# The last step of an encoder block: where the scale factors of the second half lie, and how the output is grouped

## The chip, the cores and the metric

The kernel runs on one core of a Trainium2 chip. The metric is the device time of one execution in microseconds. The core has five engines that the profile names: TensorE (PE; its weight loads are PEld), VectorE (DVE), ScalarE (ACT), GpSimd (POOL) and SyncE (SP, which here only issues transfers). Each has its own queue of instructions and they meet through semaphores.

## The reference

One layer of an encoder with a sequence of 512 and a width of 1024, in float32. A gated convolution and an attention branch are merged, a channel mixer follows, and a last RMS norm ends it. Cut to what the change touches:

```python
def rms_norm(x, g):
    x32 = x.astype(jnp.float32)
    y = x32 * lax.rsqrt(jnp.mean(x32 * x32, axis=-1, keepdims=True) + EPS)
    return y.astype(x.dtype) * g

def reference(x, ...):
    ...                       # branches, merge, norm, up projection and its convolution
    a, b = jnp.split(up, 2, axis=-1)
    x = x + (jax.nn.silu(a) * b) @ w_down[l]
    return rms_norm(x, norm_f_g)
```

The change is in the last line: each position's 1024 values are multiplied by the reciprocal root of their mean square.

## The kernel before

The sequence lies along the free dimension, the width along the partitions: `x1` holds eight slabs of 128 x 512. Nearly the whole program is matrix products on TensorE, each as three passes of rounded high and low parts (`mm3`, line 283; `passes`, line 301). A planner orders the instructions of an engine by their readiness, except those wrapped in `keep`, which stay in the written order among themselves on their engine. It also puts in the semaphores, and it lets only one engine at a time read or write a bank of PSUM, so that two readers of one tile in PSUM follow each other. PSUM has eight banks, called by number through `bank(i, name)`.

The end of the program works on two halves of the sequence, of 256 positions each: t = 0 and t = 1 (`halves[t]`). Slabs 0 to 5 are finished by then for both. Slabs 6 and 7 of the down projection are computed last, in the order slab 6 and 7 of the first half (`pdA`), then slab 6 and 7 of the second half (`pdB`). For each half these steps follow:

- `fin_sum` (lines 1208 to 1211): VectorE adds the product to `x1` (for the last slab of the second half the residual is already in PSUM), ScalarE takes the square and then scales the slab by the norm's weights.
- `fin_col` (line 1216) and `rstd_col` (lines 344 to 352): the squares are summed over the partitions by matmuls with a column of ones into bank 2 (first half) or 3 (second half), `pc_n` in the trace; ScalarE takes the root, VectorE the reciprocal, `rc_n`.
- `rstd_bc` (line 363): TensorE spreads the 256 reciprocal roots over all partitions, with an identity matrix, into bank 1 (first half) or 4 (second half), `pb_n` in the trace.
- `fin_out` (lines 1219 to 1232): VectorE multiplies slabs 0 to 5 with the factors in PSUM, in four instructions over 1, 2, 2 and 1 slabs. GpSimd, which works from a copy in SBUF, multiplies slabs 6 and 7; ScalarE makes that copy, `rs`. The output leaves in five transfers. In the first half SyncE issues all of them; in the second ScalarE issues the second and third.

Written out, the order at the end is:

```python
    plain7(1, 1, kall[3:6])
    fin_out(0, rcA)
    plain7(1, 1, kall[6:])
    sqB.append(fin_sum(1, 1))
    warm_on(3)
    rcB = fin_col(1, sqB)
    warm_on(6)
    fin_out(1, rcB)
```

So the first half's output stands in front of the last products of the second half. `warm_on` gives TensorE matmuls whose results are not used, into bank 5. On ScalarE the first half's copy `rs`, on line 1227, stands ahead of the square of the last slab, on line 1210. Line 1352 in the trace is the closing sequence of the program: SyncE waits for all transfers, every engine drains its own queue, and the engines exchange semaphores.

Of the kernel before, what the change touches and what calls it, by code (L numbers as in the profile page):

```python
# [10 lines left out]
AF = mybir.ActivationFunctionType  # L11
ALU = mybir.AluOpType

P = 128
D = 1024
S = 512
# [46 lines left out]
def block_kernel(ctx, tc, xT, vecs, wv, win, wmix, wo, wup, wst, wdp, outT):  # L63
# [3 lines left out]
    nc = tc.nc  # L67
# [6 lines left out]
    def keep(ins):  # L74
        return tc.keep_in_program_order(ins)

    def bank(i, name):
        return ps.tile([P, S], F32, tag=f"b{i}", name=name)
# [280 lines left out]
    def rstd_bc(rc, n, bb, name):  # L359

        pb = bank(bb, f"pb_{name}")
        for t in range(n):
            keep(nc.tensor.matmul(
                pb[:, t * P : (t + 1) * P], rc[:, t : t + 1].to_broadcast([P, P]), ident,
                start=True, stop=True,
            ))
        return pb
# [59 lines left out]
    pb = [pb_[t // 2][:, (t % 2) * 4 * HD : (t % 2 + 1) * 4 * HD] for t in range(NT)]  # L427
# [277 lines left out]
    z, e, o = (ap.tile([n, S], F32, tag="pp", name=nm, bufs=NPP) for nm in ("fz", "fe", "fo"))  # L705
# [71 lines left out]
    for i in range(n + LA):  # L777
# [10 lines left out]
        if 0 <= i - LA < n:  # L788
            pr, e, qb = units[i - LA]
# [72 lines left out]
    for j in range(KB):  # L862
# [28 lines left out]
        a, b = gs  # L891
# [8 lines left out]
    x1 = xp.tile([P, KB, S], F32, tag="x1", name="x1")  # L900
# [317 lines left out]

    def fin_out(t, rc):
        hs = halves[t]  # L1220
        pb = rstd_bc(rc, 2, (1, 4)[t], f"n3{t}")[:, : S // 2]
        rs = fp.tile([P, S], F32, tag="fu", name=f"rs{t}", bufs=3)[:, : S // 2]
        parts_ = ((0, 1), (1, 3), (3, 5), (5, 6), (6, 8))
        for a, b in parts_[:4]:
            y = x1[:, a:b, hs]
            keep(nc.vector.tensor_mul(y, y, pb.unsqueeze(1).to_broadcast([P, b - a, S // 2])))
        keep(nc.scalar.activation(rs, pb, AF.Copy))
        y = x1[:, 6:8, hs]
        keep(nc.gpsimd.tensor_mul(y, y, rs.unsqueeze(1).to_broadcast([P, 2, S // 2])))
        for g in (0, 1, 2, 3, 4):  # L1230
            a, b = parts_[g]
            keep((nc.sync, nc.scalar)[t * (g in (1, 2))].dma_start(outT[:, a:b, hs], x1[:, a:b, hs]))

    def warm_on(n):

# [10 lines left out]
    rcA = fin_col(0, sqA)  # L1246
# [10 lines that stand above are left out]
# [100 lines left out]
```

## Time and profile before

| | |
|---|---|
| time, median of 3 runs | 700.87 us (700.78 to 701.2) |
| profiled execution, its own time | 700.85 us |
| span of its trace | 699.1 us |
| TensorE busy | 688.4 us (98%) |
| VectorE, ScalarE, GpSimd busy | 506.6, 346.6, 159.6 us |
| transfers | 118.91 MB, mean 170 GB/s |
| mean granted TensorE clock | 0.996 |

Times in the trace count from the start of the span, in microseconds. A row of a timeline has the start, the length, the engine, the line, the operation, what it writes and reads, the shape and how many instructions are merged in it; in square brackets stands how long the engine was idle before it and who ended that. Lengths of merged rows reach from the first to the last of them. A row of a line or tile has the shortest, median and longest instruction in ns and when the first and the last began. "q" behind an engine's name means its instruction queue, which also issues the transfers.

### The profile page before, as it was taken

What the parts mean: (1) busy time and instruction counts of PE and PEld (TensorE: products, weight loads), DVE (VectorE), ACT (ScalarE), POOL (GpSimd) and SP (SyncE); (2) the same over time, 40 slices, a digit from 0 to 9 for tenths busy, and PEclk for the clock granted to TensorE, in tenths of its full rate; (3) what the DMA queues carried; (4) which work ended last, traced back from release to release, by engine and by line L of the source; (5) the groups of instructions that cost most, each with busy time, mean ns of one, the idle gap of its engine ahead of it and who ended that gap; (6) DMA issues with size and microseconds to landing.
All of it is one profiled execution on the core that took longest, in us unless ns stands there. A gap on an engine that the chain in (4) does not pass through costs nothing.

```text
span 699.1 us, 14571 instructions
## 1 busy us (share of the span) xinstructions
PE 688.4 (98%) x5978; PEld 686.1 (98%) x5978; DVE 506.6 (72%) x806; ACT 346.6 (50%) x551; POOL 159.6 (23%) x180
## 2 busy tenths in 40 slices
PE   9999999999999999999999999999999999999994
PEld 9999999999999999999999999999999999999994
DVE  6678777786687777764577877777775677877783
ACT  5574656555664443543445443455443345444662
POOL 5124646434011001035221212220000221200001
PEclk9999999999999999999999999999999999999998
DMA  8527877567359868758566647588675554334513
GB/s 313 184 85 204 206 153 186 132 167 177 96 143 272 254 179 241 233 183 206 144 156 175 168 111 214 144 182 224 192 225 178 147 147 99 102 99 139 161 60 121
DMA packets 54466, 118.91 MB, mean 170 GB/s; under 512 B 4960, under 2 KB 24416, under 8 KB 54400
## 3 DMA queue, kind: packets, MB, share of 16 engines
q1 hardware_dynamic: 39104, 96.55, 43.0%
q0 software_dynamic: 14576, 20.75, 18.6%
q8 instruction: 47, 0.77, 0.4%
q10 hardware_dynamic: 720, 0.69, 0.3%
q14 instruction: 19, 0.16, 0.1%
HBM read 115.80 MB, written 35.13 MB: 216 GB/s over the span
## 4 chain that ended last, share of the span: by engine, by line
PE 95%; DVE 2%; ACT 1%; issue 1%; ACTq 0%; POOLq 0%; POOL 0%; DVEq 0%
PE p_up L283 26%; PE p_in L283 14%; PE dn L301 13%; PE gs L301 8%; PE p_up L301 8%; PE p_wo L283 6%; PE yc L301 3%; PE ya L283 3%; PE pa L491 2%; PE pb L493 2%; PE p_g L283 2%; PE o L672 2%; PE tp L657 1%; PE pdA L283 1%; PE pdB L283 1%
## 5 line engine op out<-in xcount | busy, mean ns | idle before, releaser
L283 PE MATMUL p_up<-x1h,wh_up 128*128 128x256 f32 x536 | 104.8, 277 | 0.0
L283 PE MATMUL p_up<-x1l,wh_up 128*128 128x256 f32 x536 | 104.4, 276 | 0.0
L283 PE MATMUL p_up<-x1h,wl_up 128*128 128x256 f32 x536 | 104.3, 276 | 0.0
L250 ACT ACTIVATE wh_up<-raw_up 128x1024 fp32r<-128x1024 f32 x44 | 46.6, 1060 | 83.8 <-PE p_up L283 74.5
L139 POOL DMA_DIRECT2D sum<-in_wst_dram x51 | 52.7, 1108 | 125.3 <-DMA sum<-sum 89.1
L283 PEld LDWEIGHTS p_up<-x1h,wh_up 128*128 128x128 f32 x536 | 80.7, 188 | 0.5 <-issue 0.5
L283 PEld LDWEIGHTS p_up<-x1l,wh_up 128*128 128x128 f32 x536 | 80.8, 188 | 0.0
L283 PEld LDWEIGHTS p_up<-x1h,wl_up 128*128 128x128 f32 x536 | 80.6, 188 | 0.0
L254 DVE TENSOR_TENSOR wl_up<-raw_up,wh_up 128x1024 fp32r<-128x1024 f32 x44 | 54.1, 1230 | 16.1 <-ACT wh_up L250 16.1
L250 ACT ACTIVATE wh_F<-raw_F 128x1024 fp32r<-128x1024 f32 (+1 forms) x32 | 33.6, 1049 | 58.2 <-PE ya L283 25.9
L283 PE MATMUL p_in<-xgh,wh_in 128*128 128x256 f32 x288 | 56.8, 279 | 0.0
L283 PE MATMUL p_in<-xgh,wl_in 128*128 128x256 f32 x288 | 56.5, 277 | 0.1
L283 PE MATMUL p_in<-xgl,wh_in 128*128 128x256 f32 x288 | 56.4, 277 | 0.0
L989 DVE TENSOR_TENSOR fz<-p_up,rb_n 128x512 f32<-128x512 f32 x44 | 30.3, 690 | 32.4 <-PE p_up L283 32.4
L254 DVE TENSOR_TENSOR wl_F<-raw_F,wh_F 128x1024 fp32r<-128x1024 f32 (+1 forms) x32 | 38.6, 1207 | 20.0 <-ACT wh_F L250 19.3
L283 PEld LDWEIGHTS p_in<-xgh,wh_in 128*128 128x128 f32 x288 | 44.7, 188 | 0.7
L1002 POOL TENSOR_TENSOR ge<-fu,fu 128x512 f32<-128x512 f32 x11 | 17.1, 1552 | 120.2 <-DVE fu L586 107.2
L283 PEld LDWEIGHTS p_in<-xgh,wl_in 128*128 128x128 f32 x288 | 43.5, 188 | 0.3 <-DVE wl_in L254 0.3
L283 PEld LDWEIGHTS p_in<-xgl,wh_in 128*128 128x128 f32 x288 | 43.6, 188 | 0.0
L250 ACT ACTIVATE wh_P<-raw_P 128x768 fp32r<-128x768 f32 (+1 forms) x32 | 26.6, 832 | 27.3 <-PE dn L301 15.0
L301 PE MATMUL p_up<-x1h,wh_up 128*128 128x256 f32 x168 | 40.2, 276 | 0.0
L301 PE MATMUL p_up<-x1l,wh_up 128*128 128x256 f32 x168 | 40.2, 276 | 0.0
(319 smaller groups left out, 2033.1 us busy)
## 6 DMA issues: line engine op xcount, KB each, us to landing
raw_up<-in_wup_dram SPq DMA_DIRECT2D x44, 512.0 KB, 4.4
raw_F<-sum SPq DMA_DIRECT2D x31, 512.0 KB, 4.9
raw_in<-in_win_dram SPq DMA_DIRECT2D x24, 512.0 KB, 4.6
raw_P<-in_wst_dram SPq DMA_DIRECT2D x31, 384.0 KB, 3.6
sum<-in_wst_dram POOLq DMA_DIRECT2D x31, 256.0 KB, 5.7
sum<-in_wst_dram SPq DMA_DIRECT2D x15, 512.0 KB, 6.1
sum<-in_wst_dram POOLq DMA_DIRECT2D x15, 512.0 KB, 8.0
sum<-sum SPq DMA_DIRECT2D x30, 256.0 KB, 6.4
```

Of the source, the lines that this page charges most:

```text
L139: return lambda: keep(nc.gpsimd.dma_start(dst, src, accum_op=ALU.add))
L250: ins = nc.scalar.activation(hi, raw, AF.Copy)
L254: ins = nc.vector.tensor_sub(lo, raw, hi.bitcast(F32))
L283: keep(nc.tensor.matmul(out[:, cs], w, x[:, cs], start=start and i == 0 and c == 0, stop=stop and i == 2 and c == len(cut) - 1,))
L301: keep(nc.tensor.matmul(out, wl if x == 1 else wh, xl if x == 2 else xh, start=opens and bk not in seen, stop=closes and bk not in left,))
L491: keep(nc.tensor.matmul(pa[t][:, :VW], xt, w[:, :VW], start=start, stop=stop))
L493: keep(nc.tensor.matmul(pb[t], xt, w[:, VW:], start=start and t % 2 == 0, stop=stop and t % 2 == 1))
L657: keep(nc.tensor.transpose(tp[:, ks], pt[:, ks], ident))
L672: keep(nc.tensor.matmul(o[:, os_], vv[:, kb, pr, e, :], x[:, kb, cs], start=e == 0 and kb == 0 and i == 0, stop=e == 1 and kb == nk - 1 an ...
L989: nc.vector.tensor_mul(z, p, rb2)
L1002: keep(nc.gpsimd.tensor_mul(ge, a.rearrange(halves_of, h=2), b.rearrange(halves_of, h=2)))
```

## The change

`fin_out` is rewritten. In the second half the reciprocal roots are spread twice, into bank 4 for VectorE and into bank 2 for ScalarE's copy; in the first half both still read bank 1, but the copy stands in front of the multiplications instead of behind them. VectorE multiplies slabs 0 to 5 in three instructions over two slabs each. The output leaves in four transfers of two slabs. In the second half SyncE issues the first and third and ScalarE the second and fourth.

```diff
     def fin_out(t, rc):
         hs = halves[t]
-        pb = rstd_bc(rc, 2, (1, 4)[t], f"n3{t}")[:, : S // 2]
+        bks = ((1, 1), (4, 2))[t]
+        pb = rstd_bc(rc, 2, bks[0], f"n3{t}")[:, : S // 2]
+        pr = rstd_bc(rc, 2, bks[1], f"n3{t}r")[:, : S // 2] if t else pb
         rs = fp.tile([P, S], F32, tag="fu", name=f"rs{t}", bufs=3)[:, : S // 2]
-        parts_ = ((0, 1), (1, 3), (3, 5), (5, 6), (6, 8))
-        for a, b in parts_[:4]:
-            y = x1[:, a:b, hs]
-            keep(nc.vector.tensor_mul(y, y, pb.unsqueeze(1).to_broadcast([P, b - a, S // 2])))
-        keep(nc.scalar.activation(rs, pb, AF.Copy))
-        y = x1[:, 6:8, hs]
-        keep(nc.gpsimd.tensor_mul(y, y, rs.unsqueeze(1).to_broadcast([P, 2, S // 2])))
-        for g in (0, 1, 2, 3, 4):
-            a, b = parts_[g]
-            keep((nc.sync, nc.scalar)[t * (g in (1, 2))].dma_start(outT[:, a:b, hs], x1[:, a:b, hs]))
+
+        def by(e, r, g):
+            y = x1[:, 2 * g : 2 * g + 2, hs]
+            keep(e.tensor_mul(y, y, r.unsqueeze(1).to_broadcast([P, 2, S // 2])))
+
+        def copy():
+            keep(nc.scalar.activation(rs, pr, AF.Copy))
+
+        if t == 0:
+            copy()
+        for g in range(3):
+            by(nc.vector, pb, g)
+        if t:
+            copy()
+        by(nc.gpsimd, rs, 3)
+        for g in range(4):
+            keep((nc.sync, nc.scalar)[t * (g % 2)].dma_start(
+                outT[:, 2 * g : 2 * g + 2, hs], x1[:, 2 * g : 2 * g + 2, hs]
+            ))
```

## The prediction

> **What bounds the kernel now.** I read the page first, then the chain of waits for the last 20 us, then each engine's timeline there.
>
> ```profile
> span 699.1 us, 14571 instructions
> ...
> PE 95%; DVE 2%; ACT 1%; issue 1%; ACTq 0%; POOLq 0%; POOL 0%; DVEq 0%
> ```
>
> For 95% of the span TensorE is the path, and the diff touches none of that. Everything is decided in the tail, which the chain of waits shows (start, length, what):
>
> ```profile
> 685.11 0.46 PE pb_n L363 x4
> ...
> 688.10 1.28 POOL x L1229
> 689.38 3.34 issue
> 692.72 1.30 POOLq L1352
> ```
>
> The chain follows GpSimd to the end of the program (L1352 is the closing sequence), not a transfer. What the end waits for is in the rows of L1352 (the first two from 694 us on, the third from 698.3) and in a table of windows (last two columns: share of the DMA engines, GB/s):
>
> ```profile
> L1352 SPq DRAIN  x2: 7/7/7, 696.5 to 696.6; - x2
> L1352 POOLq DRAIN  x1: 5555/5555/5555, 692.7 to 692.7; - x1
> ...
> L1352 POOLq EVENT_SEMAPHORE  x4: 17/17/17, 698.3 to 699.0; - x4
> ...
> 695.00:695.50 0.50, 0.00 (x0) 0.00 (x0) 0.00 (x0) 0.00 (x0) 0.00 (x0) 0.50 1.04 373
> 695.50:695.90 0.40, 0.00 (x0) 0.00 (x0) 0.00 (x0) 0.00 (x0) 0.00 (x0) 0.50 0.46 156
> ```
>
> Output packets stop near 695.8, SyncE has seen them all by 696.6, and GpSimd's drain ends at 692.72 + 5.555 = 698.27. The final exchange of semaphores follows from 698.3 on and ends at 699.07, 0.80 later. So the drain, not the output, is last, by 1.67 us. I call the two halves of the sequence A (t = 0) and B (t = 1).
>
> **The change, step by step.** The rows of ScalarE, TensorE and VectorE:
>
> ```profile
> 687.64 0.38 ACT L1227 ACTIVATE rs<-pb_n 128x256 f32<-128x256 f32 x1 [3.40 <-DVE x L1226]
> 687.92 0.38 ACT L1210 ACTIVATE sq<-pdB 128x256 f32<-128x256 f32 x1
> 688.18 0.48 ACT L1211 ACTIVATE x<-pdB,vec 128x256 f32<-128x256 f32 x1
> 688.99 0.26 ACT L350 ACTIVATE ms_n<-pc_n,ex 128x2 f32<-128x2 f32 x1 [0.33 <-PE pc_n L344]
> 692.29 0.38 ACT L1227 ACTIVATE rs<-pb_n 128x256 f32<-128x256 f32 x1 [3.04 <-DVE x L1226]
> ```
> ```profile
> 682.99 0.50 PE L344 MATMUL pc_n<-ones,ssq 128*128 128x1 f32 x4
> 683.36 0.58 PE L344 MATMUL pc_n<-ones,sq 128*128 128x1 f32 x4
> ...
> 686.68 0.28 PE L283 MATMUL pdB<-gl,wh_dp 128*128 128x256 f32 x1
> ```
> ```profile
> 687.16 0.50 PE L344 MATMUL pc_n<-ones,ssq 128*128 128x1 f32 x4
> 688.35 0.61 PE L344 MATMUL pc_n<-ones,sq 128*128 128x1 f32 x4 [0.69 <-ACT sq L1210]
> ...
> 689.61 0.61 PE L363 MATMUL pb_n<-ident,rc_n 128*128 128x128 f32 x4
> ```
> ```profile
> 689.28 0.17 DVE L352 RECIPROCAL rc_n<-ms_n 128x2 f32<-128x2 f32 x1 [1.74 <-ACT ms_n L350]
> 690.25 1.95 DVE L1226 TENSOR_TENSOR x<-x,pb_n 128x256 f32<-128x256 f32 x4 [0.80 <-PE pb_n L363]
> ```
> ```profile
> 690.59 0.68 DVE L1226 TENSOR_TENSOR x<-x,pb_n 128x512 f32<-128x512 f32 x1
> ...
> 691.19 0.68 DVE L1226 TENSOR_TENSOR x<-x,pb_n 128x512 f32<-128x512 f32 x1
> ```
>
> *1. Half A's copy in front (t = 0).* Before, ScalarE's copy of A waits for VectorE's four multiplications (3.40 us) and holds up B's last square, queued behind it: pdB's last matmul ends at 686.96, the square starts only at 687.92, and TensorE stands 0.69 us for it. Moved ahead, the copy runs when A's roots are ready, at about 685.60 to 685.98; ScalarE is idle then. The price goes to VectorE: one bank, so its multiplications wait for the copy and start at 686.00 instead of about 685.6. Three of 128x512 at a pitch of 0.60 (690.59 to 691.19) end at 686.00 + 2 x 0.60 + 0.68 = 687.88. Queued behind them on VectorE is B's reciprocal; who waits for that is in step 2. A's GpSimd multiplication runs from 686.06 instead of 688.10.
>
> *2. B starts earlier.* The square runs at 687.00 to 687.38; 0.05 later (before: 688.30 to 688.35) TensorE could take it, at 687.43. TensorE is next free at 687.16 + 0.37 = 687.53 (the step from 682.99 to 683.36, half A's same eight matmuls back to back), so it sets the time: sums done at 687.53 + 0.58 = 688.11 instead of 688.96, **0.85 us earlier**. Square root 688.14, reciprocal 688.43 (VectorE is free from 687.88, slack 0.55), B's roots spread from 688.76 to 689.37. Bounds: nothing gained if the square still came late, 0.85 at most since TensorE is then full; I take 0.85, as half A's row shows that pace.
>
> *3. A second bank for B.* The added spread costs TensorE four more matmul records at a pitch of (0.61 - 0.28) / 3 = 0.11, so 0.45 us, behind the first four; VectorE doesn't wait for them. The second bank is ready at 689.82. Bank 2 held half A's column sums (matmuls to 683.94), which nothing reads any more, so it is free. VectorE's three multiplications start 0.03 behind the spread, as before (690.25 against 690.22), at 689.40, and end at 690.08, 690.68 and 691.28. The copy runs at 689.86 to 690.24 instead of at 692.29, beside VectorE's multiplications, and no longer waits for them: the 3.04 us go.
>
> *4. GpSimd's multiplication in B.*
>
> ```profile
> 692.75 1.26 POOL L1229 TENSOR_TENSOR x<-x,rs 128x512 f32<-128x512 f32 x1 [3.38 <-ACT rs L1227]
> 694.04 0.38 SPq L1232 DMA_DIRECT2D out_dram<-x  x1
> ```
> ```profile
> L603 POOL TENSOR_TENSOR z<-z,cc x4: 1292/1294/1295, 68.5 to 163.9; 128x512 f32<-128x512 f32 x4
> ```
> ```profile
> L913 POOL TENSOR_TENSOR ssq<-ssq,sq x7: 1842/1864/1866, 308.3 to 340.9; 128x512 f32<-128x512 f32 x7
> ```
> ```profile
> 105.67 0.70 DVE L633 CUSTOM_DVE_ANT_0 s<-s,strip 128x512 f32<-128x512 f32 x1 [0.23 <-PE s L629]
> ```
> ```profile
> 308.30 0.75 DVE L959 SCALAR_TENSOR_TENSOR x1l<-x,vec,x1h 128x512 fp32r<-128x512 f32 x1
> ```
>
> It starts 0.08 after the copy (692.67 to 692.75), so at 690.32, and now VectorE works beside it. The trace has the same shape at 1.29 (L603, beside VectorE work with one operand in PSUM, such as L633) and at 1.86 (L913, beside L959, whose tensors are all in SBUF). The bounds are 1.26 and 1.86. L1226 reads one operand from PSUM, so L603 is nearest and I keep 1.26: end at 691.58 instead of 694.01, **2.43 us earlier**. With 1.86 it would be 1.83.
>
> The Trainium skill ("GPSIMD Engine Reference", "Key points") says that GpSimd contends with VectorE instructions in a 2-port perf mode or with two SBUF inputs; "SBUF — State Buffer" ("SBUF: two separate sides") calls the shared pair an "exclusive lock". By that rule L1226 takes no lock and the 2.43 stand; a reader who counted L1226 as two-input would get 1.83. L603 and L913 agree with the rule.
>
> *5. Output in four groups of two slabs.* In B the issues follow VectorE's three ends and GpSimd's: SyncE 690.11, ScalarE 690.71, SyncE 691.31, ScalarE 691.61; last before: 694.04. ScalarE's two issues stand behind its copy and hold nothing up. Half A's last issue on SyncE, behind the third (687.92), is over near 688.7, so its packets are through by about 690.4, before B's. A group of 262 KB needs 0.70 us at 373 GB/s. If packets start 0.95 after the issue (694.04 to 695.0, before's last group), four groups run from 691.06 to 693.86 without a gap, so transfers bind there and end 1.9 us earlier than 695.8. SyncE would be done at 694.7 instead of 696.6. Fewer issues (eight, not ten) save nothing on the path.
>
> *6. The end.* The drain ended 4.26 us after GpSimd's multiplication (694.01 to 698.27). If that distance stays, it ends at 691.58 + 4.26 = 695.84, still behind SyncE's 694.7, and the span at 696.64. The bounds of the distance: zero, when SyncE's 694.7 + 0.80 makes 695.5, and no upper one in the trace.
>
> **Sum.** 699.07 - 2.43 = 696.64. The profiled execution took 700.85, 1.75 more than its span of 699.1, and lies 0.02 below the median of 700.87. So 696.64 + 1.75 = **698.4 us**, -0.35%. This kernel's time can be told from no change by about 0.2%, 1.4 us, so from 699.47 down.
>
> **The rivals.**
>
> *The landing sets the drain (0.18).* If GpSimd's drain ends 1.67 us after SyncE has seen the output (696.6 to 698.27), and not by GpSimd's own work, the gain is the transfers' 1.9: **698.95**. For it: transfers ran until 695.8 during the drain. Against: no row shows GpSimd waiting for a transfer there.
>
> *GpSimd and VectorE in each other's way (0.12).* 1.86 instead of 1.26: 0.60 more, **699.0**. L603 speaks against it.
>
> *Half A's copy doesn't come ahead in ScalarE's queue (0.06).* If it is placed behind the last square and its scaling (to 687.74 at the earlier start), the copy ends at 688.1, the multiplications of A at 690.0, the reciprocal behind them at 690.2 and B's roots 1.5 us later than in step 2: **699.9**, no change that can be told. Against: the copy's operands are ready 1.4 us before the square's.
>
> *The change doesn't do what it says (0.04).* If the copy of B still waited for VectorE: VectorE ends at 691.28, copy to 691.75, GpSimd to 693.1, 0.9 gained: **700.0**. The wait before was between two readers of one bank; with two banks I see nothing to make it.
>
> *The drain isn't constant (0.08, both ways).*
>
> ```profile
> L1343 POOLq DRAIN  x1: 177/177/177, 0.3 to 0.3; - x1
> ```
>
> At the start of the program GpSimd's drain took 0.18 us (0.3 to 0.5 us), at the end 5.55; the trace has no third of that kind. If it falls so that SyncE is last, the span is 695.5 and the time **697.2** (0.04). If it grows, for instance since it now starts while more transfers run, the change loses: from 4.26 + 2.43 + 1.4 = 8.1 us after the multiplication the kernel is slower by over 0.2%; a drain twice as long, 11.1 us from 690.28, gives 701.4 + 0.80 + 1.75 = **703.9** (0.04). For it: only that its length is unexplained. Against: transfers ran beside it before as well.
>
> **How the numbers follow.** The forecast has 0.52; landing 0.18, contention 0.12, the shorter and the longer drain 0.04 each, the copy in the wrong place 0.06, no effect 0.04. Faster: 0.52 + 0.18 + 0.12 + 0.04 = 0.86; same 0.06 + 0.04 = 0.10; slower 0.04. The range 697.8 to 699.5 takes in the forecast, landing and contention, and the forecast with only part of step 2 (without it, 699.25); it leaves out both drains, the wrong place and no effect (0.18).
>
> **What would show it.** Right: ScalarE's copy of A at 685.6 with B's square at 687.0; no wait of TensorE for the square; four more pb_n records in B; the copy of B about 0.5 us after VectorE's start; GpSimd's multiplication at 1.26 to 1.3, ending near 691.6; the last issue on ScalarE; the drain about 4.26 after GpSimd. Wrong: the drain ending with SyncE's landing; L1229 in B over 1.6; VectorE's L1226 over 0.68; an ACT copy still released by L1226 in B; or a changed order of instructions ahead of 680 us, which the diff gives no cause for.

## The result, and the profile after

The changed kernel takes **698.46 us** (median of 6 executions, 698.34 to 698.48) against 700.91 us before (6 executions, 700.78 to 701.2). That is 2.45 us less; the ratio is 0.9964, with a 95% interval of 0.9952 to 0.9977. The profiled execution took 698.34 us with a span of 696.6. The forecast was 698.4 us.

The chain of waits at the end of the changed kernel (start, length, what):

```profile
685.04 0.46 PE pb_n L363 x4
...
685.53 0.39 ACT rs L1231
685.92 0.07 issue
685.99 1.30 POOL x L1228
687.29 2.92 issue
690.21 1.30 POOLq L1363
```

VectorE is no longer in it: half A's copy and GpSimd's multiplication follow the spread directly. The 2.92 us called "issue" are the time in which GpSimd waits for the copy of B (its row below says 2.95, released by `rs`), and the chain's last piece is the closing drain, which GpSimd's queue takes up just before that multiplication starts. GpSimd's second multiplication starts 2.5 us earlier than before. ScalarE's timeline shows both edits, and TensorE's and VectorE's what follows from them:

```profile
685.53 0.39 ACT L1231 ACTIVATE rs<-pb_n 128x256 f32<-128x256 f32 x1 [1.35 <-PE pb_n L363]
686.93 0.38 ACT L1210 ACTIVATE sq<-pdB 128x256 f32<-128x256 f32 x1 [1.02 <-PE pdB L283]
687.21 0.47 ACT L1211 ACTIVATE x<-pdB,vec 128x256 f32<-128x256 f32 x1
688.07 0.26 ACT L350 ACTIVATE ms_n<-pc_n,ex 128x2 f32<-128x2 f32 x1 [0.39 <-PE pc_n L344]
689.78 0.38 ACT L1231 ACTIVATE rs<-pb_n31r 128x256 f32<-128x256 f32 x1 [1.45 <-PE pb_n31r L363]
```
```profile
687.09 0.50 PE L344 MATMUL pc_n<-ones,ssq 128*128 128x1 f32 x4
687.45 0.58 PE L344 MATMUL pc_n<-ones,sq 128*128 128x1 f32 x4
...
688.69 0.61 PE L363 MATMUL pb_n<-ident,rc_n 128*128 128x128 f32 x4
689.14 0.61 PE L363 MATMUL pb_n31r<-ident,rc_n 128*128 128x128 f32 x4
```
```profile
685.94 1.88 DVE L1228 TENSOR_TENSOR x<-x,pb_n 128x512 f32<-128x512 f32 x3 [1.57 <-ACT rs L1231]
688.37 0.17 DVE L352 RECIPROCAL rc_n<-ms_n 128x2 f32<-128x2 f32 x1 [0.54 <-ACT ms_n L350]
689.34 1.88 DVE L1228 TENSOR_TENSOR x<-x,pb_n 128x512 f32<-128x512 f32 x3 [0.80 <-PE pb_n L363]
```

B's last square is now released by TensorE's own last product and no longer stands behind a copy; the eight sum matmuls run back to back, as half A's do; the second spread lies 0.45 us behind the first; and the copy of B waits for that spread, not for VectorE. GpSimd, and the closing sequence (now line 1363):

```profile
685.99 1.30 POOL L1228 TENSOR_TENSOR x<-x,rs 128x512 f32<-128x512 f32 x1 [54.87 <-ACT rs L1231]
690.24 1.27 POOL L1228 TENSOR_TENSOR x<-x,rs 128x512 f32<-128x512 f32 x1 [2.95 <-ACT rs L1231]
```
```profile
L1363 SPq DRAIN  x2: 7/7/7, 694.7 to 694.7; - x2
L1363 POOLq DRAIN  x1: 5560/5560/5560, 690.2 to 690.2; - x1
...
L1363 POOLq EVENT_SEMAPHORE  x4: 17/17/17, 695.8 to 696.5; - x4
```

GpSimd's multiplication ends at 690.24 + 1.27 = 691.51, its drain at 690.21 + 5.56 = 695.77, 4.26 later as before. SyncE had seen all output at 694.74, so the drain is still last, by 1.0 us. The windows of the same stretch (last two columns: share of the DMA engines, GB/s) show that the output is now bound by its rate, with the DMA engines' share at 1 and above:

```profile
691.00:692.00 1.00, 0.00 (x0) 0.00 (x0) 0.22 (x1) 0.00 (x0) 0.51 (x1) 1.00 1.08 381
692.00:693.00 1.00, 0.00 (x0) 0.00 (x0) 0.00 (x0) 0.00 (x0) 0.00 (x0) 1.00 1.08 379
693.00:693.50 0.50, 0.00 (x0) 0.00 (x0) 0.00 (x0) 0.00 (x0) 0.00 (x0) 1.00 1.11 387
```

### The profile page after: what moved, and what is told of

Its sections match the earlier page's. It is cut to its first block, busy times and chain, and to the rows that moved or that the text cites. A ratio compares the mean times of both kernels' runs of the same rounds, so it can differ in the third digit from the quotient of the medians.

```text
span 696.6 us, 14572 instructions
## 1 busy us (share of the span) xinstructions
PE 687.8 (99%) x5982; PEld 685.6 (98%) x5982; DVE 506.6 (73%) x804; ACT 346.7 (50%) x551; POOL 159.6 (23%) x180
## 4 chain that ended last, share of the span: by engine, by line
PE 94%; DVE 2%; ACT 1%; issue 1%; DMA 1%; ACTq 0%; SPq 0%; POOLq 0%; POOL 0%; DVEq 0%
PE p_up L283 26%; PE p_in L283 14%; PE dn L301 13%; PE gs L301 8%; PE p_up L301 8%; PE p_wo L283 6%; PE yc L301 3%; PE ya L283 3%; PE p_g L283 2%; PE o L672 2%; PE pa L491 2%; PE pb L493 1%; PE tp L657 1%; PE pdA L283 1%; PE pdB L283 1%
```

## The experiments

Two theories stood against each other. Mine: GpSimd's last multiplication plus a constant drain of 4.26 us sets the end. The rival: the landing of the output sets it, and the drain follows the landing. A second question was what share each edit has. Times are medians; those of before, taken beside them, lie between 700.84 and 700.89 us.

### The edits one by one

**Half A's copy ahead, alone** (on the kernel before):

```diff
+        if t == 0:
+            keep(nc.scalar.activation(rs, pb, AF.Copy))
         for a, b in parts_[:4]:
 ...
-        keep(nc.scalar.activation(rs, pb, AF.Copy))
+        if t:
+            keep(nc.scalar.activation(rs, pb, AF.Copy))
```

> The kernel before with one edit: in half A the copy stands in front of the multiplications. My theory (GpSimd's last multiplication plus a drain of 4.26 us sets the end): B's square starts at 687.0 instead of 687.9, all of B comes 0.85 to 0.9 us earlier, GpSimd's multiplication of B ends near 693.15: 700.0 us. Rival (the last landing sets the end): the last issue also comes 0.85 earlier, the same 700.0, so this run tells only the share of this part. Rival (the copy ahead is worth nothing by itself, since A's multiplications start later and hold up B's reciprocal): 700.8.

Measured: 700.03 us, ratio 0.9988 (0.9979 to 0.9997). The copy and GpSimd's multiplication of B:

```profile
691.53 0.38 ACT L1230 ACTIVATE rs<-pb_n 128x256 f32<-128x256 f32 x1 [3.04 <-DVE x L1228]
```
```profile
691.99 1.26 POOL L1232 TENSOR_TENSOR x<-x,rs 128x512 f32<-128x512 f32 x1 [4.55 <-ACT rs L1230]
```

B comes 0.76 us earlier in this trace (in which TensorE reached the tail 0.08 us later), and still pays the 3.04 us behind VectorE. The copy ahead is worth 0.86 us of the time by itself (700.89 - 700.03). The delay of A's multiplications costs nothing: B's reciprocal still finds VectorE idle, for 0.47 us.

**The second bank, alone** (on the kernel before):

```diff
+        pr = rstd_bc(rc, 2, 2, f"n3{t}r")[:, : S // 2] if t else pb
 ...
-        keep(nc.scalar.activation(rs, pb, AF.Copy))
+        keep(nc.scalar.activation(rs, pr, AF.Copy))
```

> The kernel before with one edit: B's roots are spread a second time into bank 2, which the copy reads; five groups and A's order as before. My theory: B starts when it did, the copy of B runs at 690.7 instead of 692.3, GpSimd ends near 692.43 instead of 694.01, 1.58 earlier, and the end follows it: 699.3 us. Rival (the landing sets the end): the transfers are bound by their rate from about 692.2 on, 0.92 MB at 373 GB/s, so they land about 1.1 earlier: 699.8. If the parts add up, this and the copy ahead make 2.43.

Measured: 699.29 us, ratio 0.9979 (0.997 to 0.9988), 1.60 us (700.89 - 699.29). The landing rival had 699.8.

```profile
690.72 0.38 ACT L1228 ACTIVATE rs<-pb_n31r 128x256 f32<-128x256 f32 x1 [1.45 <-PE pb_n31r L363]
```
```profile
691.18 1.27 POOL L1230 TENSOR_TENSOR x<-x,rs 128x512 f32<-128x512 f32 x1 [1.80 <-ACT rs L1228]
```

The copy waits for its own spread only. The two parts make 0.86 + 1.60 = 2.46 us; the whole change measured 700.91 - 698.46 = 2.45.

**Four groups, alone** (on the kernel before):

```diff
-        parts_ = ((0, 1), (1, 3), (3, 5), (5, 6), (6, 8))
-        for a, b in parts_[:4]:
+        parts_ = ((0, 2), (2, 4), (4, 6), (6, 8))
+        for a, b in parts_[:3]:
 ...
-        for g in (0, 1, 2, 3, 4):
+        for g in range(4):
 ...
-            keep((nc.sync, nc.scalar)[t * (g in (1, 2))].dma_start(...))
+            keep((nc.sync, nc.scalar)[t * (g % 2)].dma_start(...))
```

> The kernel before with one edit: three multiplications of two slabs and output in four groups, second and fourth of B on ScalarE. My theory: only VectorE's 1.88 us instead of 1.95 counts, twice on the path (A's copy and B's copy wait for it): 0.1 us, 700.75 to 700.85. Rival (the grouping brings a part of the gain by itself, since the output is moved in larger pieces): over 0.3 us, 700.5 or less.

Measured: 700.81 us, ratio 1.0002 (0.9993 to 1.001), no difference that can be told. The 0.1 us that I expected lies within the noise, so the grouping has no share of the gain that shows; the other two parts account for all of it.

### What sets the end

**One bank in B, copy first** (on the changed kernel):

```diff
-        pr = rstd_bc(rc, 2, bks[1], f"n3{t}r")[:, : S // 2] if t else pb
+        pr = pb
 ...
-        if t == 0:
-            copy()
+        copy()
         for g in range(3):
             by(nc.vector, pb, g)
-        if t:
-            copy()
```

> The changed kernel, but without the second bank: in B as in A ScalarE copies first from the one bank and VectorE starts behind the copy. My theory: the copy starts with the first spread (689.35) instead of 0.45 later, GpSimd ends 0.45 earlier (691.06), VectorE 0.41 later (691.63); the drain still ends after the landing, so 0.45 faster than the changed kernel: 698.0 us. Rival (the landing sets the end): the transfers start 0.41 later, 698.85.

Measured: 698.0 us, ratio to the kernel before 0.9957 (0.9944 to 0.9971).

```profile
689.87 1.27 POOL L1228 TENSOR_TENSOR x<-x,rs 128x512 f32<-128x512 f32 x1 [2.51 <-ACT rs L1231]
```
```profile
689.82 1.88 DVE L1228 TENSOR_TENSOR x<-x,pb_n 128x512 f32<-128x512 f32 x3 [1.22 <-ACT rs L1231]
```
```profile
L1360 SPq DRAIN  x2: 7/7/7, 695.2 to 695.2; - x2
...
L1360 POOLq DRAIN  x1: 5567/5567/5567, 689.8 to 689.8; - x1
```

Here the landing is later than in the changed kernel (SyncE 695.24 against 694.74) and GpSimd earlier (691.13 against 691.51). The time went with GpSimd: 0.46 us less (698.46 - 698.0). Its drain ends at 695.40, with SyncE 0.15 ahead of it.

**No GpSimd work in B** (on the changed kernel; VectorE multiplies slabs 6 and 7 of B too):

```diff
-        pr = rstd_bc(rc, 2, bks[1], f"n3{t}r")[:, : S // 2] if t else pb
+        pr = pb
 ...
-        if t:
-            copy()
-        by(nc.gpsimd, rs, 3)
+        if t:
+            by(nc.vector, pb, 3)
+        else:
+            by(nc.gpsimd, rs, 3)
```

> The changed kernel, but VectorE multiplies all eight slabs of B, in four instructions; no copy, no second bank and no GpSimd work in B. My theory: GpSimd is done at 687.3 and its drain at 691.6, so SyncE's landing becomes last: VectorE ends near 691.8, the transfers are still bound by their rate from 691.0 on, SyncE is through near 694.75 and the span ends 0.8 later, near 695.5: 697.3 us. Rival (the drain follows the landing by 1.0 to 1.7 us whoever works): the landing is hardly moved, so 698.4 or more. Rival (VectorE's fourth multiplication makes the last group late): last issue 691.85 instead of 691.54, 698.7.

Measured: 697.29 us, ratio 0.9948 (0.9935 to 0.9962).

```profile
L1364 SPq DRAIN  x2: 7/7/7, 694.7 to 694.8; - x2
L1364 POOLq DRAIN  x1: 5596/5596/5596, 686.0 to 686.0; - x1
```

GpSimd's drain is over at 686.00 + 5.60 = 691.60, 3.2 us ahead of SyncE. So the drain does not follow the landing, and that rival falls. SyncE is through at 694.77, where it was in the changed kernel, and yet the span is 1.0 us shorter. VectorE's last group is issued 0.4 us later than GpSimd's was, but the transfers are bound by their rate, so it costs nothing.

**GpSimd twice in B** (on the changed kernel, an instruction whose result nothing reads):

```diff
         by(nc.gpsimd, rs, 3)
+        if t:
+            sc = fp.tile([P, S], F32, tag="fu", ...)
+            keep(nc.gpsimd.tensor_mul(sc, x1[:, 0:2, hs], rs...))
```

> The changed kernel with one instruction more: behind its multiplication of B, GpSimd makes another of the same shape into a tile that nothing reads. No output waits for it. My theory: GpSimd ends 1.25 us later and the end moves with it: 699.7 us. Rival (the landing sets the end): 698.45, no change. Rival (the drain's 4.26 us are counted from the time it is taken up and not from GpSimd's last operation, 5.56 us in all): it is taken up as the last operation starts, so 699.7 as well.

Measured: 699.69 us, ratio 0.9983 (0.9974 to 0.9992), 1.23 us more than the changed kernel, though no output waits for the instruction.

```profile
691.67 1.26 POOL L1242 TENSOR_TENSOR sc<-x,rs 128x512 f32<-128x512 f32 x1
```
```profile
L1366 SPq DRAIN  x2: 7/7/7, 694.9 to 694.9; - x2
...
L1366 POOLq DRAIN  x1: 6699/6699/6699, 690.5 to 690.5; - x1
```

The drain was taken up during the first multiplication and is 6.70 us long instead of 5.56; it ends at 697.18, 4.26 behind the second one. So the 4.26 us count from GpSimd's last operation, and the 5.56 are no fixed length. SyncE was through 2.3 us before it. The drain's end against GpSimd's and SyncE's in eight traces, worked out from such rows (the last is the trace of the run without any GpSimd work in the tail, described below):

| kernel | GpSimd's last operation ends | its drain ends | difference | SyncE through | span ends |
|---|---|---|---|---|---|
| before | 694.02 | 698.27 | 4.26 | 696.61 | 699.07 |
| copy ahead | 693.25 | 697.51 | 4.26 | 695.84 | 698.31 |
| second bank | 692.45 | 696.71 | 4.26 | 695.55 | 697.51 |
| changed | 691.51 | 695.77 | 4.26 | 694.74 | 696.57 |
| one bank, copy first | 691.13 | 695.40 | 4.26 | 695.24 | 696.19 |
| GpSimd twice | 692.92 | 697.18 | 4.26 | 694.92 | 697.98 |
| no GpSimd in B | 687.33 | 691.60 | 4.26 | 694.77 | 695.54 |
| no GpSimd in A or B | 632.96 | 637.22 | 4.26 | 696.36 | 697.13 |

The span ends 0.77 to 0.80 us behind whichever of drain and SyncE is later. (The ends are rounded one by one, so that their difference can be off by 0.01.)

### Contention between VectorE and GpSimd

**VectorE multiplies from SBUF in B** (on the kernel with one bank and the copy first):

```diff
-            by(nc.vector, pb, g)
+            by(nc.vector, rs if t else pb, g)
```

> The kernel with one bank and the copy first, but in B VectorE also multiplies by the copy in SBUF and no longer by the roots in PSUM, so that all its tensors are in SBUF while GpSimd works. Theory (the two contend only when VectorE reads two operands from SBUF): GpSimd's multiplication is held up, by one of VectorE's instructions (1.9 us) up to all of them (3.1 us), and the end moves with it, 0.6 to 1.8 us above the kernel with one bank. Rival (no contention in either form): GpSimd's multiplication stays at 1.27 and the time is that of the kernel with one bank.

Measured: 698.83 us, ratio 0.9968 (0.9956 to 0.9981), 0.83 us more than its partner with PSUM.

```profile
690.38 1.75 DVE L1228 TENSOR_TENSOR x<-x,rs 128x512 f32<-128x512 f32 x1
```
```profile
689.82 1.77 POOL L1228 TENSOR_TENSOR x<-x,rs 128x512 f32<-128x512 f32 x1 [2.52 <-ACT rs L1231]
```
```profile
L1360 SPq DRAIN  x2: 7/7/7, 696.2 to 696.2; - x2
...
L1360 POOLq DRAIN  x1: 6066/6066/6066, 689.8 to 689.8; - x1
```

The partner's rows stand under "One bank in B, copy first". With both operands in SBUF the two engines take turns: GpSimd is 0.5 us longer (1.77 instead of 1.27), VectorE's second multiplication takes 1.75 instead of 0.68, and its three take 2.96 in all instead of 1.88. The price lies in the forecast band, but the way differs from what I expected: GpSimd's multiplication stayed under the 1.9 us that I gave as the least, and it was VectorE that lost over 1 us, so its last group is late, SyncE is through at 696.25 and the landing is last, not the drain (695.85). With one operand in PSUM, as in the partner, neither shows any of this. The Trainium skill ("SBUF — State Buffer", "SBUF: two separate sides") says that whoever starts first holds the pair "for the whole instruction" and the other blocks; these rows agree, with VectorE's first multiplication ahead of GpSimd's and its second behind.

### A version faster than both

Without GpSimd in B the landing is last, so I started the output earlier. **B in five groups of 1, 2, 2, 2, 1 slabs** (on the kernel without GpSimd in B):

```diff
+        parts_ = (((0, 2), (2, 4), (4, 6), (6, 8)), ((0, 1), (1, 3), (3, 5), (5, 7), (7, 8)))[t]
 ...
+        for a, b in parts_[: 3 + 2 * t]:
+            by(nc.vector, pb, a, b)
```

> The kernel without GpSimd in B, with B in five groups of 1, 2, 2, 2 and 1 slabs (first, third and fifth on SyncE). There the landing of the output is last. My theory: the transfers of B are bound by their rate, so they end as much earlier as they start earlier: VectorE is through with one slab 0.26 us before two, all else follows, 0.26 less than the kernel without GpSimd in B: 697.0 us. Rival (the last issue sets the landing, not the rate): VectorE's last multiplication ends 0.1 later (five instructions), the last issue at 692.0: no change or 0.1 more, 697.3 to 697.4.

Measured: 697.16 us, ratio 0.9947 (0.9933 to 0.996). The windows of this kernel:

```profile
690.50:691.00 0.50, 0.00 (x0) 0.00 (x0) 0.50 (x2) 0.00 (x0) 0.00 (x0) 1.00 0.67 238
691.00:692.00 1.00, 0.00 (x0) 0.00 (x0) 0.90 (x2) 0.00 (x0) 0.00 (x0) 0.64 0.74 261
692.00:693.00 1.00, 0.00 (x0) 0.00 (x0) 0.00 (x0) 0.00 (x0) 0.00 (x0) 0.50 1.11 388
```

Packets start before 691, but the first group of one slab is through before the second group's packets start (none starts between 691.15 and 691.3), and the rate between 691 and 692 is 261 GB/s, where the kernel without GpSimd in B has 374. In the two traces the span is 0.23 us shorter (695.31 against 695.54). The medians differ by 0.13 us, less than the spread of the kernel without GpSimd in B (697.03 to 697.4), so neither the expected 0.26 us nor any gain at all is shown.

**GpSimd and the copy out of half A as well**:

```diff
-        if t == 0:
-            keep(nc.scalar.activation(rs, pr, AF.Copy))
-        for a, b in parts_[: 3 + 2 * t]:
+        for a, b in parts_:
             by(nc.vector, pb, a, b)
-        if t == 0:
-            by(nc.gpsimd, rs, 6, 8)
```

> The same with GpSimd and ScalarE's copy left out of half A as well; VectorE multiplies all eight slabs of both halves. My theory: GpSimd's drain was over long before the end already, and A's multiplications end at 688.1, ahead of B's reciprocal at 688.4, so nothing changes: 697.0 us, as the run before it in this list. Rival (GpSimd's drain still costs something at the end, or VectorE is late for B's reciprocal): a difference of 0.2 us or more, either way.

Measured: 697.19 us, ratio 0.9952 (0.994 to 0.9965): the same as the run before it, as far as can be told. One of the five executions took 698.92 us, the other four 697.09 to 697.31. The trace is that of the 698.92 us execution; it reached the tail 1.8 us later than the run before it, ahead of anything that this edit touches. The simplest program, with neither copy, second bank nor GpSimd at the end, is 1.27 us faster than the changed kernel.

Its trace also shows more about the drain. GpSimd's last operation is now an earlier multiplication, on another line, and the closing drain is taken up there:

```profile
631.35 1.61 POOL L1002 TENSOR_TENSOR ge<-fu,fu 128x512 f32<-128x512 f32 x1 [9.91 <-DVE fu L586]
```
```profile
L1354 POOLq DRAIN  x1: 5901/5901/5901, 631.3 to 631.3; - x1
```
```profile
632.96:634.00 1.04, 1.04 (x12) 1.04 (x11) 0.85 (x2) 0.85 (x2) 0.00 (x1) 1.00 0.00 0
634.00:635.00 1.00, 1.00 (x12) 1.00 (x11) 0.96 (x3) 0.00 (x0) 0.00 (x0) 1.00 0.00 0
```

It ends 4.26 us behind that multiplication too, 59 us before SyncE is through, and in the first 2 us of that wait no transfer ran. So the 4.26 us need neither the landing nor this one multiplication, and nothing in the traces ties them to the transfers.

## Why the prediction was right

The time was forecast as 698.4 and came as 698.46. By its steps:

1. *The copy of A in front.* Forecast 685.60 to 685.98, measured 685.53 to 685.92; A's multiplications were to end at 687.88 and ended at 687.82. In this execution TensorE reached the tail 0.07 us earlier, which lies ahead of anything the change touches; with that added back, the row is on the forecast.
2. *B earlier by 0.85.* TensorE no longer waits for the square and starts its second four sum matmuls at 687.45, where 687.53 was forecast. Alone it was worth 0.86 us. The reciprocal found VectorE idle (0.54 us, forecast slack 0.55).
3. *The second bank.* The copy of B was forecast at 689.86 and ran at 689.78; 0.45 us behind the first spread. Alone 1.60 us, where steps 3 and 4 implied 1.58.
4. *GpSimd's multiplication.* 1.26 kept, 1.27 measured. The choice of L603 as the nearest row held. The experiment from SBUF supports the reason why L913 was not the nearest: VectorE works beside it on tensors that are all in SBUF, and with that arrangement GpSimd's multiplication took 1.77 here. Contention as a rival falls.
5. *Four groups.* Forecast to land with SyncE through at 694.7; it was at 694.74, at 379 to 387 GB/s. Alone, the grouping showed no difference (700.81).
6. *The end.* The constant 4.26 us was an extrapolation from a single trace, and the step with the most doubt. It was 4.26 in every trace. The prediction gave no reason why it should stay, so that this step came right was in part luck; the experiments bore it out only afterwards. What the drain does in these 4.26 us no run shows. Nor does every drain of GpSimd take so long: the one at the start of the program, which the prediction names, ended at 0.49 us, 0.05 behind the last of four small writes of constants (the prediction's "no third of that kind" misses two more, of 0.10 and 0.05 us, in the closing exchange). What makes the difference stays open.

The rivals: the landing (698.95) is excluded by the runs with no and with two GpSimd multiplications in B. The distance from GpSimd's last multiplication to the end of the drain neither grew nor shrank. ScalarE's order and the release of the copy came out as the diff says.

## What to carry to other kernels

Ask which engine's closing drain ends last, not only when the output lands: here GpSimd's last instruction cost its own time and another 4.26 us, and a GpSimd multiplication placed last to relieve VectorE was dearer than giving VectorE the work. In this program, whose planner lets only one engine at a time at a bank of PSUM, two readers of one bank are a queue. Spreading a small result twice (0.45 us of an idle TensorE) removes the wait; putting the shorter reader first leaves 0.4 us of it, for the other reader, and was the better of the two here (698.0 against 698.46). An instruction that waits early in an in-order queue charges everything behind it, so look at who stands behind a wait before asking whether the wait itself matters.

## What the runs showed of the hardware

- GpSimd's closing drain ended 4.26 us behind GpSimd's last operation (a multiplication of 128x512 in each case) in all eleven traces, wherever in the program that operation stood; VectorE's, TensorE's and ScalarE's ended within 0.2 us of their last instruction, which for ScalarE was the issue of a transfer.
- A VectorE and a GpSimd multiplication that both read two operands from SBUF held each other up, in the one trace that has them side by side: 1.75 us instead of 0.68 for VectorE's blocked instruction, 1.77 instead of 1.27 for GpSimd's. With one of VectorE's operands in PSUM, both ran at full pace side by side.
